# Three transfers for weight sums per half block, begun ahead of DeltaNet's first keys, with the out-projection's groups between those of the pairs

## The chip, the cores and the metric

The kernel runs on one core of a Trainium2 chip. The metric is the device time of one execution in microseconds (us); of several runs the median counts. Engines are named as in the profile: PE is TensorE's matmuls, PEld its weight loads, DVE VectorE, ACT ScalarE, POOL GpSimd, SP SyncE. ACTq and POOLq are the queues through which ScalarE and GpSimd issue transfers; those that GpSimd issues are called software transfers here (q0 on the page).

## The reference

One layer of a hybrid decoder trunk: 512 tokens and 16 meta tokens of width 2048, normalised, go through one input projection, whose columns feed three mixers on disjoint heads; their gated outputs are concatenated and go through one output projection, with a residual and a last norm.

```
h = rms_norm(x, norm_w); h = pad(h)
proj = h @ w_in
dq, dk, dv, dz, db, da, gq, gk, gv, gz, gl, fq, fk, fv, fz, ff = split_cols(proj)
o_dn  = gated_delta_rule_chunked(silu(conv(dq)), silu(conv(dk)), silu(conv(dv)), ...)   # 6 heads x 128
o_gla = gla_chunked(gq, gk, gv, log_g)                                                   # 5 heads
o_fox = forgetting_attention(fq, fk, fv, log_f)                                          # 5 heads x 128
o = concat(gated(o_dn, dz), gated(o_gla, gz), o_fox * silu(fz))
return rms_norm(x + o @ w_out, final_norm_w)
```

## The kernel before, in words

**Projection.** All of x stays on chip, transposed, as a high and a low part (xh, xl). The weights of one head's projection come in two half blocks of 128 x 1024 floats. `load_half` (L145) loads one on SyncE's queue (raw), ScalarE casts it to whi (L166), VectorE takes the rest as wlo (L167), and TensorE multiplies in three parts (whi by xh, whi by xl, wlo by xh; L223). The first four gates (dz) are done in quarters of the weights while x itself still comes in (L265, L277).

**Sums of weights.** For seven pairs of blocks of the forgetting heads (`PAIRS`, L428), and for four groups of the output projection, the kernel multiplies by sums of blocks in place of single blocks, to save products. These sums are formed in DRAM without an engine: software transfers copy a block (L438) or add one to it (L436, an accumulating transfer). A pair fills ti with 4 copies of 256 KB, 2 sums of input weights and 2 sums of ti into ti, the last ones each waiting for earlier ones. A group of the output projection fills tw with the same numbers at 512 KB each. That makes 56 and 32, or 88 transfers. Pairs are numbered from -1 to -7 in the table below, groups of the output projection from 0 to 3.

**What sets the place of the transfers.** `jobs` (L454) appends the transfers of the groups given to it to the list `chores`, stage by stage: first all copies of all groups given, then the first sums, then the others. After each half block `load_half` takes `rate[0]` transfers from the list. The transfers are also ordered behind the split of that half block (`paced`, L171), but only for the program's order; no semaphore makes them wait for it. On the chip a software transfer starts as soon as GpSimd comes to it in its own order and its own waits (for a free slot, or for the transfer that it adds to) are over. `AHEAD` (L1195) is the table: at a point (g, i) of the program, read by `ahead` (L1199), a number sets the rate and a tuple appends groups.

**The stages.** The program goes through DeltaNet's heads in two groups g of three (L1206): gates (`gate_z`), keys (`dn_keys`), values, queries, the inverse of the chunk matrices (`dn_inverse`) and the mix over four blocks (`dn_mix`); then GLA's gates and heads, the five forgetting heads, and the output projection. A point (g, -1) of the table lies between gates and keys, (g, 0) between keys and values. The projections of later stages fill TensorE while the small products of a stage wait for other engines, so inverse and mix of a group lie beside the projections that follow.

**Names and lines that the steps below touch.** In `dn_keys`, gb is a broadcast load of 792 KB on ScalarE's queue, which VectorE reads (L657). In `dn_inverse`, the matrix ab goes to DRAM as sc (L721) and comes back as iv and xm (L724, L726), all three on ScalarE's queue; ScalarE then copies uf (L754). In `dn_mix`, each block loads eg (L834, ScalarE's queue), takes its exponential (L835), copies its last column to egl (L837, VectorE), and multiplies it by q (L838, GpSimd); pks (L842), zz (L845, VectorE), py (L849), y (L851, ScalarE) and psn (L855) follow. In GLA, pss (L983) is a row of 64 tiny products. GpSimd also does the first step of each SiLU (L350: stdz for DeltaNet's gates, stc for its keys, values and queries, stgz for GLA's gates) and memsets (gsc L132 and L133, pb L593, ab L699 and L711, uf L751).

Of the kernel before, what the change touches and what calls it, by code (L numbers as in the profile page):

```python
# [83 lines left out]
def tile_hybrid_trunk(ctx, tc, xT, xtok, mtok, w_gate, w_in, w_out, w_dn, consts, lmask, fin_w, out, dbg=None):  # L84
# [1107 lines left out]

    SUMS = {h: [(h, 0), (h, 1)] for h in range(4)}
    XLAST = 0
    AHEAD = {(0,0):(2,(-1,-2,-3,-4),(-5,-6,-7),(0,1,2,3))}  # L1195
    XSUM = {1: (0,), 2: (1,2), 9:(3,)}
    PM = (308, 319)

    def ahead(g, i):  # L1199
        for n in AHEAD.get((g, i), ()):  # L1200
            if isinstance(n, tuple):
                jobs(*[in_jobs(-k - 1) if k < 0 else out_jobs(k) for k in n])
            else:
                rate[0] = n
# [313 lines left out]
```

## Time and profile before

| | |
|---|---|
| median of 3 runs | 1012.02 us (1011.39 to 1012.87) |
| profiled execution | 1008.45 us |
| its span | 1006.7 us |
| TensorE busy | 988.8 us, 98% |
| VectorE, ScalarE, GpSimd busy | 643.2, 460.5, 247.7 us |
| software transfers (q0) | 31.46 MB, 15.2% of the time of 16 DMA engines |

The span is the time from the first to the last instruction of the profiled execution. In rows of a timeline the first number is the start in us from the span's start, the second the duration, then engine, line, operation, out<-in, and in brackets the idle time of the engine ahead of it with what ended it. In rows of waits stand total, times and longest. In rows of windows stand, after the window, the time span and each engine's busy time with its count of instructions, then the clock granted to TensorE, the DMA engines' busy share, and GB/s.

### The profile page before, as it was taken

The page shows a single profiled execution, that of the slowest core. Times are in us where ns is not written, and L with a number is a line of the kernel's source. Part 1 is how long each engine was busy: PE and PEld are TensorE (multiplying, and loading weights), DVE is VectorE, ACT ScalarE, POOL GpSimd, SP SyncE. Part 2 cuts the span into 40 slices and gives each one's busy share as a digit, 9 for nine tenths or more (in the row PEclk, how much of TensorE's full clock was granted, in tenths as well). Part 3 has the DMA queues.
Part 4 walks back from the last instruction along what each step waited for, and adds up shares of the span by engine and source line. Part 5 has one row for each costly group of instructions (what it writes and reads, how often), then busy time and mean ns, then how long its engine had stood idle before and what let it go on. Part 6 is the DMA issues. An engine that isn't in the chain of part 4 may idle for free.

```text
span 1006.7 us, 19781 instructions
## 1 busy us (share of the span) xinstructions
PE 988.8 (98%) x7866; PEld 906.6 (90%) x7866; DVE 643.2 (64%) x1389; ACT 460.5 (46%) x1041; POOL 247.7 (25%) x280
## 2 busy tenths in 40 slices
PE   9999999999999999998999999999999999999996
PEld 8899999899999888898989988899999998888885
DVE  7366877965566894244576774866474667677673
ACT  7654533434456244143445453555444444444454
POOL 0022533322313334123042620311112123000060
PEclk9999999999999999999999999999999999999999
DMA  9625357655446577456847221243333375457534
GB/s 345 235 67 158 129 174 155 154 137 146 146 118 157 123 213 247 154 122 145 216 107 174 65 74 64 74 137 124 116 117 129 119 241 176 146 168 231 178 114 168
DMA packets 62402, 152.57 MB, mean 152 GB/s; under 512 B 12925, under 2 KB 16173, under 8 KB 62052
## 3 DMA queue, kind: packets, MB, share of 16 engines
q1 hardware_dynamic: 36912, 108.22, 32.5%
q0 software_dynamic: 11136, 31.46, 15.2%
q10 hardware_dynamic: 14260, 11.61, 4.0%
q8 instruction: 62, 1.02, 0.4%
q14 instruction: 32, 0.26, 0.1%
HBM read 143.99 MB, written 38.60 MB: 181 GB/s over the span
## 4 chain that ended last, share of the span: by engine, by line
PE 51%; DVE 2%; issue 0%; ACT 0%; ACTq 0%; DVEq 0%
PE pp L223 13%; PE pp_a L533 6%; PE pa L1295 5%; PE pq L1295 4%; PE pt L1295 4%; PE pp_d L533 3%; PE pp_c L533 3%; PE pp_b L533 3%; PE ps L1295 2%; PE pss L983 1%; PE pr L1295 1%; PE pfo L1186 1%; PE pfa L1153 1%; PE pfx L1170 1%; PE pgo L1046 0%; PE pfd L1154 0%
## 5 line engine op out<-in xcount | busy, mean ns | idle before, releaser
L223 PE MATMUL pp<-xl,whi 128*128 128x264 f32 (+2 forms) x1120 | 284.6, 306 | 0.0
L223 PE MATMUL pp<-xh,whi 128*128 128x264 f32 (+2 forms) x1120 | 282.7, 305 | 1.5 <-DVE fqk L341 0.8
L223 PE MATMUL pp<-xh,wlo 128*128 128x264 f32 (+2 forms) x1120 | 282.6, 305 | 1.4 <-issue 0.9
L223 PEld LDWEIGHTS pp<-xh,whi 128*128 128x128 f32 x1120 | 186.4, 188 | 11.2 <-DVE fqk L341 1.0
L223 PEld LDWEIGHTS pp<-xh,wlo 128*128 128x128 f32 x1120 | 186.6, 189 | 10.7 <-issue 1.4
L223 PEld LDWEIGHTS pp<-xl,whi 128*128 128x128 f32 x1120 | 187.1, 189 | 8.9 <-issue 0.2
L167 DVE TENSOR_TENSOR wlo<-raw,whi 128x1024 fp32r<-128x1024 f32 (+1 forms) x124 | 129.9, 1058 | 87.2 <-ACT whi L166 77.4
L166 ACT CAST whi<-raw 128x1024 fp32r<-128x1024 f32 (+1 forms) x124 | 109.9, 902 | 164.4 <-PE pp L223 122.5
L350 POOL TENSOR_SCALAR stc<-cv 128x528 f32<-128x528 f32 (+1 forms) x18 | 28.1, 1559 | 117.0 <-DVE cv L598 95.5
L598 DVE SCALAR_TENSOR_TENSOR cv<-pb,cpk,cv 128x528 f32<-128x528 f32 (+1 forms) x54 | 41.0, 760 | 0.7
L1319 POOL TENSOR_TENSOR acc<-acc,fw 128x512 f32<-128x512 f32 x4 | 6.3, 1592 | 127.1 <-ACT sqf L1316 127.1
L162 ACT ACTIVATE whi<-raw 128x512 fp32r<-128x512 f32 x35 | 20.5, 624 | 25.3 <-PE pp_c L533 7.9
L166 ACT CAST whis<-raws 128x1024 fp32r<-128x1024 f32 x16 | 16.4, 1049 | 27.4 <-DMA raws<-tw 15.4
L163 DVE SCALAR_TENSOR_TENSOR wlo<-raw,whi 128x512 fp32r<-128x512 f32 x35 | 23.0, 685 | 8.7 <-ACT whi L162 8.6
L1295 PE MATMUL pa<-wloo,oh 128*128 128x512 f32 x72 | 28.4, 395 | 0.0
L1295 PE MATMUL pa<-whio,ol 128*128 128x512 f32 x72 | 28.4, 395 | 0.0
L341 DVE TENSOR_TENSOR pb<-pp,rstd 128x264 f32<-128x264 f32 (+1 forms) x36 | 13.7, 423 | 22.3 <-PE pp L223 22.2
L533 PE MATMUL pp_a<-xh,whi 128*128 128x264 f32 (+1 forms) x112 | 27.9, 282 | 0.0
L533 PE MATMUL pp_a<-xl,whi 128*128 128x264 f32 (+1 forms) x112 | 27.7, 281 | 0.0
L167 DVE TENSOR_TENSOR wlos<-raws,whis 128x1024 fp32r<-128x1024 f32 x16 | 19.3, 1221 | 11.4 <-ACT whis L166 11.4
L1295 PE MATMUL pa<-whio,oh 128*128 128x512 f32 x72 | 25.9, 400 | 0.0
L838 POOL TENSOR_TENSOR eg<-eg,qT 128x384 f32<-128x384 f32 x8 | 8.5, 1058 | 70.2 <-DVE egl L837 70.2
(499 smaller groups left out, 2256.4 us busy)
## 6 DMA issues: line engine op xcount, KB each, us to landing
raw<-in_w_in SPq DMA_DIRECT2D x96, 512.0 KB, 3.9
tw<-in_w_dn POOLq DMA_DIRECT2D x24, 512.0 KB, 6.4
ti<-in_w_in POOLq DMA_DIRECT2D x42, 256.0 KB, 4.7
raw<-ti SPq DMA_DIRECT2D x14, 512.0 KB, 4.1
rawo<-in_w_out SPq DMA_DIRECT2D x13, 512.0 KB, 3.3
raws<-tw SPq DMA_DIRECT2D x12, 512.0 KB, 4.5
raw<-in_w_in SPq DMA_DIRECT2D x21, 256.0 KB, 3.1
xt<-in_xtok SPq DMA_DIRECT2D x8, 512.0 KB, 8.6
```

The costliest lines, as they stand in the source:

```text
L162: pace[0] = A.activation(hi, raw, AF.Copy, scale=-1.0).ins
L163: pace[1] = V.scalar_tensor_tensor(out=lo, in0=raw, scalar=-1.0, in1=hi.bitcast(F32), op0=ALU.mult, op1=ALU.subtract).ins
L166: pace[0] = A.copy(hi, raw).ins
L167: pace[1] = V.tensor_tensor(out=lo, in0=raw, in1=hi.bitcast(F32), op=ALU.subtract).ins
L223: mm = PE.matmul(p_[:, :nt], wt[:, j * m : (j + 1) * m], xx[k][:, t0 : t0 + nt], start=(k == 0 and wt is hi and xx is xh), stop=(k == KT - ...
L341: V.tensor_tensor(out=o, in0=p_[rows], in1=rstd[rows, t0 : t0 + n], op=ALU.mult)
L350: G.tensor_scalar_max(t, src, LOW)
L533: m = PE.matmul(p_[:, cols], wt[:, j * P : (j + 1) * P], xx[j][part_][:, cols], start=first and i == 0, stop=last and i == len(todo) - 1, ...
L598: V.scalar_tensor_tensor(out=c, in0=pb[:, t0 + w : w + T], scalar=cwc[:, blk, w : w + 1], in1=c, op0=ALU.mult, op1=ALU.add)
L983: mm = PE.matmul(ps[o0 : o0 + n, b * n : b * n + n], kx[rr, k0 : k0 + n], qx[rr, q0 : q0 + n], start=True, stop=True)
L1153: PE.matmul(pa[:, :m], qT[:, ts], kT[:, :m], start=True, stop=True)
L1295: PE.matmul(p_, o_[:, s], w_, start=(first and n == 0), stop=(last and n == 2), skip_group_check=True)
```

## The change

```
-    AHEAD = {(0,0):(2,(-1,-2,-3,-4),(-5,-6,-7),(0,1,2,3))}
+    AHEAD = {(0,-1):(3,(-1,-2,-3,-4),(0,1),(-5,-6,-7),(2,3))}
```

The list of transfers is opened ahead of DeltaNet's first keys instead of behind them, six half blocks earlier (the keys of three heads). Three transfers are taken per half block instead of two. The groups stand in another order: pairs -1 to -4, then groups 0 and 1 of the output projection, then pairs -5 to -7, then groups 2 and 3. The transfers themselves are the same 88. The orders of TensorE and SyncE are unchanged; ScalarE and VectorE have neighbours swapped in some places.

GpSimd at the start of the program, before (gsc are the last memsets of the constants, stdz the first gates of DeltaNet, stc its first keys):

```order
L132 MEMSET gsc 128x1
L133 MEMSET gsc 128x4
L350 TENSOR_SCALAR stdz_567<-zdz_564 128x512
L350 TENSOR_SCALAR stdz_576<-zdz_573 128x512
L350 TENSOR_SCALAR stdz_585<-zdz_582 128x512
L350 TENSOR_SCALAR stdz_594<-zdz_591 128x512
L593 MEMSET pb_710 128x3
L350 TENSOR_SCALAR stc_829<-cv_824 128x528
L593 MEMSET pb_835 128x3
L438 DMA ti<-in_w_in 128x512 x2
L350 TENSOR_SCALAR stc_954<-cv_949 128x528
L593 MEMSET pb_960 128x3
```

And after, at the same place:

```order
L132 MEMSET gsc 128x1
L133 MEMSET gsc 128x4
L438 DMA ti<-in_w_in 128x512 x3
L350 TENSOR_SCALAR stdz_567<-zdz_564 128x512
L350 TENSOR_SCALAR stdz_576<-zdz_573 128x512
L350 TENSOR_SCALAR stdz_585<-zdz_582 128x512
L438 DMA ti<-in_w_in 128x512 x2
L350 TENSOR_SCALAR stdz_594<-zdz_591 128x512
L593 MEMSET pb_710 128x3
L438 DMA ti<-in_w_in 128x512 x5
L350 TENSOR_SCALAR stc_834<-cv_829 128x528
L593 MEMSET pb_840 128x3
```

The first copies of ti stood behind the first keys' SiLU; now three stand ahead of the first gate's, behind memsets that wait for no transfer, and ten stand ahead of the first keys'.

GpSimd in the first group's values and queries and the first keys' start of the second group, after (stc are values and queries, stdz gates of the second group, pb the start of its keys; before, transfers of ti stand here):

```order
L438 DMA tw<-in_w_dn 16x8192 x2
L350 TENSOR_SCALAR stc_1957<-cv_1952 128x512
L438 DMA tw<-in_w_dn 16x8192
L711 MEMSET ab_2092 51x32
L436 DMA tw<-in_w_dn 256x512 x4
L350 TENSOR_SCALAR stc_2086<-cv_2081 128x512
L436 DMA tw<-tw 256x512
L350 TENSOR_SCALAR stdz_2703<-zdz_2700 128x512
L436 DMA tw<-tw 256x512 x3
L350 TENSOR_SCALAR stdz_2776<-zdz_2773 128x512
L593 MEMSET pb_2783 128x3
L438 DMA ti<-in_w_in 128x512 x5
```

The first 16 transfers of the output projection's weights, at 512 KB each, have come here from the second group.

GpSimd from the second group's inverse to its mix, before (stgz are GLA's gates, uf and b the inverse's end, kq GLA's first memsets, eg the mix's four blocks):

```order
L350 TENSOR_SCALAR stgz_5029<-zgz_5026 128x512
L751 MEMSET uf_4319 128x1536
L438 DMA tw<-in_w_dn 16x8192 x6
L761 MEMSET b_4349 64x384
L1228 MEMSET kq_5035 128x1536
L1228 MEMSET kq_5036 128x1536
L438 DMA tw<-in_w_dn 16x8192 x2
L838 TENSOR_TENSOR eg_4401<-eg_4401,qT_3749 128x384
L438 DMA tw<-in_w_dn 16x8192
L838 TENSOR_TENSOR eg_4474<-eg_4474,qT_3749 128x384
L436 DMA tw<-in_w_dn 256x512 x3
L838 TENSOR_TENSOR eg_4547<-eg_4547,qT_3749 128x384
```

And after, with the same instructions of the second group:

```order
L350 TENSOR_SCALAR stgz_5057<-zgz_5054 128x512
L751 MEMSET uf_4353 128x1536
L761 MEMSET b_4383 64x384
L1228 MEMSET kq_5063 128x1536
L1228 MEMSET kq_5064 128x1536
L838 TENSOR_TENSOR eg_4435<-eg_4435,qT_3779 128x384
L838 TENSOR_TENSOR eg_4508<-eg_4508,qT_3779 128x384
L838 TENSOR_TENSOR eg_4581<-eg_4581,qT_3779 128x384
```

The transfers between these instructions are gone; the last of all now stands ahead of the second group's inverse, between its two memsets of ab.

## Prediction

> **What bounds the kernel now.** I read the page's first part, then TensorE's own waits, largest first, then engine timelines around each.
>
> ```profile
> span 1006.7 us, 19781 instructions
> PE 988.8 (98%) x7866; PEld 906.6 (90%) x7866; DVE 643.2 (64%) x1389; ACT 460.5 (46%) x1041; POOL 247.7 (25%) x280
> ...
> q0 software_dynamic: 11136, 31.46, 15.2%
> ```
>
> ```profile
> PE py L849 <- DVE zz L845: 2.2, 1, 2.2
> ...
> PE pp L223 <- issue: 0.9, 1, 0.9
> PE pss L983 <- issue: 0.8, 1, 0.8
> ...
> PE pp L223 <- ACT whi L166: 0.7, 1, 0.7
> ...
> PE pp L223 <- DVE wlo L167: 0.5, 1, 0.5
> ```
>
> TensorE is busy for 988.8 of 1006.7 us. The change adds no matmul and takes none away, and the orders of TensorE and SyncE are the same before and after. So it can move the time only by these stalls, or by new ones. None of the 88 software transfers is on the chain that ended last, as their readers, loads of the forgetting heads and of the out-projection, come far later. What counts is **whom the transfers slow down while they run**. They move 31.46 MB in 15.2% of 1006.7 us, that is 153 us at about 205 GB/s.
>
> **What goes: the stalls of the second DeltaNet group.** Before, the 32 out-projection transfers run beside this group's inverse and mix. After, GpSimd's order has its last one ahead of the GLA gates (stgz), and so ahead of the waits that follow. The largest stall is that of py at 461.96 us:
>
> ```profile
> 440.56 0.38 ACTq L834 DMA_DIRECT2D eg<-gd  x1
> 444.05 0.53 ACT L835 ACTIVATE eg<-eg 128x384 f32<-128x384 f32 x1 [0.85 <-DMA eg<-gd]
> ```
>
> ```profile
> 445.89 2.75 POOL L436 DMA_DIRECT2D tw<-in_w_dn  x3
> ```
>
> ```profile
> 453.91 0.37 ACTq L834 DMA_DIRECT2D eg<-gd  x1
> 459.69 0.52 ACT L835 ACTIVATE eg<-eg 128x384 f32<-128x384 f32 x1 [4.91 <-DMA eg<-gd]
> ```
>
> ```profile
> 455.00:460.00 5.00, 4.80 (x42) 4.59 (x40) 0.00 (x0) 0.31 (x1) 0.00 (x0) 1.00 0.89 235
> ```
>
> The same load of eg takes 444.05 - 440.56 = 3.49 us in one block and 459.69 - 453.91 = 5.78 us in the next, when three accumulating copies of 512 KB are in flight and the DMA engines are busy to 0.89. VectorE's copy egl waits for it, zz stands behind egl in VectorE's order, and py waits for zz. The load is 2.29 us late and the stall is 2.2. Without the transfers **2.2 us** go; 0 if the delay has another cause.
>
> The next pair, whi 0.7 and wlo 0.5, stands where that group's inverse ends:
>
> ```profile
> 206.49 0.26 ACTq L721 DMA_DIRECT2D sc<-ab  x1
> 211.74 0.40 ACTq L724 DMA_DIRECT2D iv<-sc  x1
> ...
> 385.15 0.26 ACTq L721 DMA_DIRECT2D sc<-ab  x1
> ...
> 393.60 0.38 ACTq L724 DMA_DIRECT2D iv<-sc  x1
> ```
>
> ```profile
> 385.43 0.98 POOL L438 DMA_DIRECT2D tw<-in_w_dn  x2
> ```
>
> ScalarE stands at L724 until sc has landed: 211.74 - 206.49 = 5.25 us in the first group, 393.60 - 385.15 = 8.45 us here, with two copies of 512 KB issued 0.3 us after it. The gate's activations, the copies of uf and the cast of whi queue up behind. With 3.2 us back the cast is in time, and **1.2 us** go (0 to 1.2).
>
> Last the two stalls whose releaser is "issue":
>
> ```profile
> 513.57 0.39 PE L223 MATMUL pp<-xh,wlo 128*128 128x264 f32 x1 [0.86 <-issue]
> ...
> 518.32 0.32 PE L983 MATMUL pss<-kq,kq 64*32 64x32 f32 x20 [0.77 <-issue]
> ```
>
> ```profile
> 506.51 1.79 POOL L436 DMA_DIRECT2D tw<-tw  x2
> ```
>
> TensorE waits there for nothing that the profile shows, among 64 tiny matmuls at a time, with two 512 KB accumulating copies in flight. If its instructions came late because of these, both go (1.6 us); if not, none. I take half, **0.8 us**. The other rows of this view lie at the very start or among the later heads, where no software transfer runs before or after; they stay.
>
> **What comes: three copies at the very start.** The first three 256 KB copies of ti now stand on GpSimd right behind the memsets of gsc, ahead of the first activation step, and wait for nothing.
>
> ```profile
> 2.45 0.13 POOL L133 MEMSET gsc<- 128x4 bf16 x1
> 54.38 4.40 POOL L350 TENSOR_SCALAR stdz<-zdz 128x512 f32<-128x512 f32 x3 [51.80 <-DVE zdz L362]
> ```
>
> ```profile
> 0.00:5.00 5.00, 3.80 (x18) 3.80 (x19) 0.35 (x1) 2.40 (x3) 1.82 (x18) 1.00 0.61 170
> 5.00:10.00 5.00, 5.00 (x26) 4.37 (x26) 3.02 (x5) 2.79 (x6) 0.00 (x0) 1.00 0.98 334
> ```
>
> ```profile
> 7.36 0.62 ACT L166 CAST whi1q<-raw1q 128x512 fp32r<-128x512 f32 x1 [0.45 <-DMA raw1q<-in_w_in]
> 8.69 0.74 ACT L265 ACTIVATE xh<-xs,cpk 128x528 fp32r<-128x528 f32 x1 [0.71 <-DMA xs<-in_xT]
> ```
>
> ```profile
> 6.48 0.63 PE L277 MATMUL pp<-xh,wlo0q 128*128 128x512 f32 x1
> ...
> 8.30 0.40 PE L277 MATMUL pp<-xh,whi1q 128*128 128x512 f32 x1
> ...
> 10.14 0.39 PE L277 MATMUL pp<-xh,whi0q 128*128 128x512 f32 x1
> ```
>
> So they issue from 2.6 us on, into DMA engines that are soon full (0.61, then 0.98) and feed a TensorE that waits for them. 3 x 262 KB = 786 KB at 334 GB/s take 2.35 us from the loads of x and of the first weights. The cast of whi1q ends at 7.98 us and its matmul starts at 8.30: 0.32 us of slack. The xh that is ready at 9.43 us is read at 10.14: 0.71 us. So of 2.35 us, some 0.4 is absorbed: **+1.9 us**, since this stage keeps TensorE full to its end and gives nothing back. Lower bound 0.3: the three copies get only the gaps of the first 5 us, where the engines are busy to 0.61. Upper bound 4: the first matmuls take 0.63 us where later ones take 0.39, and a longer wait among the first may bring that back.
>
> What a turn between the queues would make of it: if the loads keep half of each engine while the copies run, they have lost 1.7 us by the cast at 7.36 (half of 3.4 us, if they begin at 4 us) and all 2.35 by 9.4, and less the slacks that is 1.4 and 1.6 us instead of 1.9. The Trainium skill, "DMA: Bandwidth & Descriptors" (Queues, rings and completion order), states such a rule: each DMA engine goes round the queues that it has work for and changes after a packet. No row here shows whose packet goes first, and I stay with 1.9.
>
> **What comes: a denser first group.** The 44 half blocks of transfers become 30, and the out-projection's first 16 now lie in the first DeltaNet group. GpSimd's own issue time (2.75 us for three sums, in the row above) delays the gates and values that stand behind it by less than the slacks below, and is set at nothing; without those it would be some 1 us at a place. The early places with little slack are these:
>
> ```profile
> 89.36 0.50 DVE L657 TENSOR_SCALAR atm<-gb,gcol 16x16 f32<-16x16 f32 x3 [1.06 <-DMA gb<-gd]
> ...
> 93.49 1.21 DVE L167 TENSOR_TENSOR wlo<-raw,whi 128x1024 fp32r<-128x1024 f32 x1
> ```
>
> ```profile
> 97.59 0.40 PE L223 MATMUL pp<-xh,wlo 128*128 128x264 f32 x2
> ...
> 183.72 0.40 PE L223 MATMUL pp<-xh,whi 128*128 128x512 f32 x1
> ...
> 309.75 0.38 PE L849 MATMUL py<-zz,uf 128*128 128x128 f32 x2
> ```
>
> ```profile
> 306.93 0.86 DVE L845 SCALAR_TENSOR_TENSOR zz<-pks,cols,vp 128x128 f32<-128x128 f32 x3
> ```
>
> ```profile
> 178.79 1.05 ACT L166 CAST whi<-raw 128x1024 fp32r<-128x1024 f32 x1 [5.17 <-DMA raw<-in_w_in]
> ...
> 183.69 1.05 ACT L166 CAST whi<-raw 128x1024 fp32r<-128x1024 f32 x1 [1.25 <-PE pp L223]
> ...
> 304.95 0.52 ACT L835 ACTIVATE eg<-eg 128x384 f32<-128x384 f32 x1 [0.51 <-DMA eg<-gd]
> ```
>
> - gb at 89 us: VectorE waits for it, and the split wlo stands behind. TensorE reads that wlo at 97.6 us, 2.9 us after its end at 94.7. Six copies and a sum are in flight where there were two copies.
> - the weights cast at 178.8 us, which land just then: four accumulating copies of 512 KB now run beside them. Their matmul starts at 183.7, 3.9 us after the cast ends.
> - sc at 206 us: three accumulating copies of tw and then five of ti are now near it. At 3.2 us more, as at 385 us, the casts behind it are just in time.
> - eg at 305 us: five copies of 512 KB now stand there. At 2.29 us more, as at 454 us, it eats a slack of 2 us: zz ends at 307.8 us, py starts at 309.75.
>
> Each is between 0 (the slack holds) and 1.8 us: the worst delay seen, 3.2 us, half as much again because three transfers run where two did, less a slack of 3. All four lie nearer to nothing, since each slack about equals the delay seen: 0.3 us each, **+1.2 us**.
>
> Sum: 1.9 + 1.2 - 2.2 - 1.2 - 0.8 = -1.1 us on the span, 1005.6. The profiled execution took 1008.45 us, 1.75 more than its span and 3.57 less than the median of the runs, 1012.02; against that median the forecast is **1010.9 us**.
>
> **The rivals.** About 0.2%, or 2 us, is what a measurement of this kernel can tell from no change.
> - **The start is free and the late stalls go.** The early copies take the gaps, the four places hold. 0.3 - 2.2 - 1.2 - 1.6 = -4.7: 1007.3 us. For it: the DMA engines have 0.39 of the first 5 us free. Against it: 0.98 right after.
> - **The crowded first group starves TensorE.** Mechanism: the latency-bound loads eg, gb and sc wait behind denser software traffic, as eg did at 454 us, and with slacks of 2 to 3 us each delay over 3 us is a stall. It decides once three transfers per half block pile up: three of 512 KB take 7.7 us at 205 GB/s, and the casts of two half blocks start 4.9 us apart (178.79 and 183.69). Then three of the four places cost their 1.8 beside the start's 1.9 and the 4.2 that go: 5.4 + 1.9 - 4.2 = +3.1, **1015.1 us**; with all four and the start at 4 us, 1019.0.
> - **Nothing changes on the path.** The start absorbs the copies (0.3) and the late stalls have other causes (egl's place in VectorE's order, ScalarE's queue), and come back: 1012.3 us.
>
> **How the numbers follow.** The forecast (each term within about 1 us, 1009 to 1013) gets 0.40, the free start 0.22, the crowded group 0.28, nothing 0.10. Faster by over 2 us (below 1010.0): all of the free start and a third of the forecast, 0.36. Slower by over 2 us (above 1014.0): nearly all of the crowded group and a little of the forecast, 0.30. Within: 0.34. The range takes in the free start with the spread of its terms and the crowded group up to the middle of its two times: 1006.7 to 1016.5.
>
> **What would show it.** The first three ti copies issue before 5 us, and the matmul of whi1q starts near 10 us; the first work of GpSimd behind them, at 54.4 us before, starts 1.9 us later. The wait of py for zz is gone, eg lands in 3.5 us in every block of the second group, L724 follows L721 by 5 us there, and the "issue" stalls at 513 and 518 us are gone or, if they are not, had nothing to do with transfers. New waits of TensorE for wlo near 97 us, whi near 183 and 217 us or zz near 309 us are the crowded group's. The forecast is wrong if the first stage is not delayed, or if one of these is over 1 us.

## The result and the profile after

The changed kernel takes **1020.46 us** (median of 6 runs, 1019.06 to 1021.98) against 1012.09 us of the kernel before (6 runs, 1009.19 to 1015.17): a ratio of 1.0084, 95% interval 1.0063 to 1.0104. It is slower by about 8.4 us, where 1.1 us less was forecast. The ratios here and below are those of the comparison with its interval, and can differ a little from the quotient of the medians. The profiled execution is that of 1019.06 us.

The page's head and TensorE's own waits, after (total, times, longest):

```profile
span 1017.4 us, 19780 instructions
PE 993.1 (98%) x7866; PEld 908.3 (89%) x7866; DVE 641.1 (63%) x1389; ACT 460.7 (45%) x1041; POOL 249.5 (25%) x280
...
q0 software_dynamic: 11136, 31.46, 14.9%
```

```profile
PE pm L735 <- DVE iv L729: 4.3, 2, 3.9
PE pss L983 <- issue: 1.9, 1, 1.9
PE pp L277 <- ACT whi2q L166: 1.6, 1, 1.6
PE pp L223 <- DVE wlo L167: 1.2, 3, 0.5
```

The software transfers move the same bytes in the same share of time. The wait of py is gone from the list, as forecast. At its head stands one that the list of before didn't have: pm, which waits for iv, in the first group's inverse. TensorE's busy time is also up by 4.3 us, with the same 7866 matmuls.

Since TensorE's order is the same in both kernels, each matmul can be set against its twin, and the difference of their start times, from one span's start to the other's, is a step curve that shows where the 10.6 us came from (the medians differ by 8.4: the profiled execution of before lies 3.6 us under its median, that of after 1.4 under its own):

```
place in the kernel (us of before)         steps, us    sum, us
start, casts of whi1q and whi2q (8 to 11)    +2.40       +2.40
pk behind gb (100 to 122)                    +1.08       +3.48
pm, first inverse (221 to 232)               +6.45       +9.95
mix of the first group (235 to 345)          +0.20      +10.15
whi, wlo, second inverse (348 to 388)        +2.37      +12.52
whi, wlo at 400                              -0.23      +12.29
py and what is near it (430 to 474)          -1.90      +10.39
GLA's pss (513 to 518)                       +0.13      +10.52
the rest                                     +0.12      +10.64
```

**The first inverse.** ScalarE's and VectorE's timelines there, after; the answering rows of before are 206.49 and 211.74:

```profile
213.44 0.26 ACTq L721 DMA_DIRECT2D sc<-ab  x1
...
219.34 0.40 ACTq L724 DMA_DIRECT2D iv<-sc  x1
```

```profile
227.51 0.58 DVE L729 STREAM_TRANSPOSE iv<-iv 128x384 f32<-128x384 f32 x1 [9.44 <-DMA iv<-sc]
```

```profile
216.59 1.62 POOL L438 DMA_DIRECT2D ti<-in_w_in  x3
219.37 1.39 POOL L751 MEMSET uf<- 128x1536 f32 x1 [1.15 <-DMA sc<-ab]
220.69 1.04 POOL L438 DMA_DIRECT2D ti<-in_w_in  x2
```

```profile
228.14 1.49 PE L735 MATMUL pm<-iv,an 32*32 32x32 f32 x48 [3.86 <-DVE iv L729]
```

iv comes back 227.51 - 219.34 = 8.17 us after its load is issued, with five copies of ti in flight from GpSimd's rows; before, the transpose starts at 214.41 us, 2.67 us behind its load. The trip begins late, too: L721 stands 6.95 us later than before, 3.5 of which the whole kernel was late by then. Altogether iv is 9.6 us later than that shift, and TensorE waits 3.86 us for it. The windows right behind (2 us each; the last three numbers are the granted clock, the DMA share and GB/s) show what the wait costs beyond itself:

```profile
226.00:228.00 2.00, 0.00 (x0) 0.00 (x0) 0.49 (x1) 0.00 (x0) 0.00 (x0) 0.76 0.08 24
228.00:230.00 2.00, 1.86 (x50) 1.79 (x51) 1.85 (x8) 1.79 (x4) 0.00 (x0) 0.50 0.00 0
230.00:232.00 2.00, 2.00 (x11) 2.00 (x11) 1.96 (x4) 1.19 (x3) 0.00 (x0) 0.50 0.00 0
232.00:234.00 2.00, 2.00 (x11) 2.00 (x11) 1.43 (x2) 0.00 (x0) 0.38 (x1) 0.53 0.90 246
```

Behind the idle stretch the clock that TensorE was granted is at half up to about 234 us, nearly 6 us after pm has started, and this gives the other 2.5 of the step's 6.45 us.

**The start.** GpSimd issues the three copies at 2.49 us, and whi2q comes late:

```profile
2.49 1.87 POOL L438 DMA_DIRECT2D ti<-in_w_in  x3
56.79 4.42 POOL L350 TENSOR_SCALAR stdz<-zdz 128x512 f32<-128x512 f32 x3 [52.42 <-DVE zdz L362]
```

```profile
12.84 0.50 PE L277 MATMUL pp<-xh,whi2q 128*128 128x512 f32 x1 [1.60 <-ACT whi2q L166]
```

stdz starts at 56.79 instead of 54.38 us: the 2.4 us stay to the end of the stage. The next step is gb, which VectorE had at 89.36 us before:

```profile
94.12 0.50 DVE L657 TENSOR_SCALAR atm<-gb,gcol 16x16 f32<-16x16 f32 x3 [3.42 <-DMA gb<-gd]
```

**The second inverse and mix.** The inverse's first trip (L702 to L707 on ScalarE's queue) and the eg that had been late, after:

```profile
348.75 1.98 ACTq L702 DMA_DIRECT2D scr<-an  x4
350.84 0.28 ACTq L708 DMA_DIRECT2D ab<-scmeta  x1
357.65 0.32 ACTq L707 DMA_DIRECT2D ab<-scr  x1
358.02 1.99 ACT L166 CAST whi<-raw 128x1024 fp32r<-128x1024 f32 x2 [12.83 <-DMA scr<-an]
```

```profile
344.85 0.89 POOL L436 DMA_DIRECT2D tw<-tw  x1 [1.95 <-DMA tw<-tw]
349.90 0.88 POOL L436 DMA_DIRECT2D tw<-tw  x1 [2.84 <-DMA tw<-tw]
```

```profile
466.40 0.37 ACTq L834 DMA_DIRECT2D eg<-gd  x1
470.11 0.52 ACT L835 ACTIVATE eg<-eg 128x384 f32<-128x384 f32 x1 [2.84 <-DMA eg<-gd]
```

L707 follows L702 by 8.90 us, where it was 5.54 before (338.60 to 344.14), with the last two 512 KB sums of tw in flight; two casts of weights stand behind it on ScalarE. That is a place that the prediction didn't have. The eg is back at 3.71 us, and py no longer waits.

### The profile page after: what moved, and what is told of

Its sections match the earlier page's. It is cut to its first block, busy times and chain, and to the rows that moved or that the text cites. A ratio compares the mean times of both kernels' runs of the same rounds, so it can differ in the third digit from the quotient of the medians.

```text
span 1017.4 us, 19780 instructions
## 1 busy us (share of the span) xinstructions
PE 993.1 (98%) x7866; PEld 908.3 (89%) x7866; DVE 641.1 (63%) x1389; ACT 460.7 (45%) x1041; POOL 249.5 (25%) x280
## 4 chain that ended last, share of the span: by engine, by line
PE 51%; DVE 2%; issue 0%; ACT 0%; ACTq 0%; DVEq 0%
PE pp L223 13%; PE pp_a L533 6%; PE pa L1295 5%; PE pq L1295 4%; PE pt L1295 4%; PE pp_d L533 3%; PE pp_c L533 3%; PE pp_b L533 3%; PE ps L1295 2%; PE pss L983 1%; PE pr L1295 1%; PE pfo L1186 1%; PE pfa L1153 1%; PE pfx L1170 1%; PE pgo L1046 0%
## 5 line engine op out<-in xcount | busy, mean ns | idle before, releaser
L350 POOL TENSOR_SCALAR stc<-cv 128x528 f32<-128x528 f32 (+1 forms) x18 | 30.6, 1699 | 120.2 <-DVE cv L598 96.3
L162 ACT ACTIVATE whi<-raw 128x512 fp32r<-128x512 f32 x35 | 20.5, 624 | 25.4 <-PE pp_c L533 10.6
L351 ACT ACTIVATE stc<-stc 128x528 f32<-128x528 f32 (+1 forms) x18 | 11.5, 638 | 33.0 <-POOL stc L350 21.0
```

Source lines behind the costliest of these rows:

```text
L162: pace[0] = A.activation(hi, raw, AF.Copy, scale=-1.0).ins
L350: G.tensor_scalar_max(t, src, LOW)
L351: A.activation(t, t, AF.Exp, scale=-1.0)
```

## The experiments

**The theory**: the time is lost where small loads on ScalarE's queue make a round trip (ab, sc and iv of the inverses, gb, eg) while software transfers are in flight, and at the start. **Rivals**: the early opening shifts everything and is the whole cause; the rate of three is; the out-projection's new place is; the neighbours that swapped on VectorE are (splits of weights that moved ahead of inverse steps).

Medians in us, ratios to the kernel before with intervals. "Step" means the step curve of the run's profile against the first profile of before; where TensorE's order differs a little from that of before, the matmuls are set against each other by their position.

### One part of the change at a time

```
a1_early    AHEAD = {(0,-1):(2,(-1,-2,-3,-4),(-5,-6,-7),(0,1,2,3))}
a2_rate3    AHEAD = {(0,0):(3,(-1,-2,-3,-4),(-5,-6,-7),(0,1,2,3))}
a3_order    AHEAD = {(0,0):(2,(-1,-2,-3,-4),(0,1),(-5,-6,-7),(2,3))}
a4_nostart  AHEAD = {(0,0):(3,(-1,-2,-3,-4),(0,1),(-5,-6,-7),(2,3))}
```

a1_early, expected: 

> The kernel before with the list opened ahead of the first keys, but still two transfers per half block and the groups in the old order. Theory (round trips: the change loses time where small latency-bound loads on ScalarE's queue run beside software transfers, plus the copies at the very start): two copies of 256 KB at the start cost two thirds of the 2.4 us that three cost, +1.6; the inverse of the first group sees two transfers per half block as before, so its stall of 4 us and more does not come, 0 to +2; the stalls of the second group stay. In all +1.5 to +4 us. Rival (the early opening is the whole cause, since everything behind is shifted): +8 to +10 us. Rival (the rate of three is the cause): within 0.5 us of before.

Measured: **1007.51, ratio 0.9949 (0.9928 to 0.9970): faster than before**. Steps: +1.08 at the start, +1.4 near 100 us, +1.7 at pm of the second inverse, then -2.2 at py and -1.0 at 513 us. The early opening alone is no loss; that rival falls. The theory's own forecast for this run, 1.5 to 4 us slower, was missed too: it had left the stalls of py and at 513 us in place.

a2_rate3, expected: 

> The kernel before with three transfers per half block, opened behind the first keys as before, old order. Theory (round trips): no copies at the start, 0; ten copies of ti stand around the return of iv in the first group's inverse, so TensorE's wait for pm near 221 us comes, +3 to +6; the waits for py at 462 us and at 400 us go, -2 to -3.3. In all +0 to +4 us. Rival (early opening is the cause): -2 to -3 us. Rival (the place of the out-projection's groups is the cause): -2 to -3 us.

Measured: 1017.31, ratio 1.0045 (1.0027 to 1.0063). That is about 4.6 us, a little above the expected 0 to 4, and the place was not the expected one: the first inverse's trip stayed at 5.3 and 2.7 us, with next to nothing in flight beside it. Instead +1.8 at 173 us, +3.2 at py of the first mix (290 us, eg 8.75 us on its way), +8.1 at the second inverse's first trip (L702 to L707 11.0 us), and -2.3 at the old py. So at a rate of three, in the old order, stalls come; where they come depends on which transfers stand beside which trip.

a3_order, expected: 

> The kernel before with only the order of the groups changed: out-projection 0 and 1 ahead of pairs -5 to -7, two per half block from behind the first keys. Theory (round trips): nothing changes up to 240 us, so no stall at the first inverse; 512 KB transfers then run beside the first group's mix (eg), where slack is 2 us, 0 to +2; transfers of 256 KB run beside the second inverse and mix, where 512 KB ones did, so that the 2.2 us of py shrink, 0 to -2. In all -2 to +2 us. Rival (the place of the out-projection's groups is the cause): +5 to +10 us.

Measured: 1011.28, ratio 0.9999 (0.9978 to 1.0020). The first inverse is untouched (+0.2 up to 260 us), the first mix loses 2.0 (eg 7.21 us on its way), pm of the second inverse 1.4, and py gives back 2.3. The new order alone is no loss either.

a4_nostart, expected: 

> The changed kernel with the list opened behind the first keys as before, so that no copy stands at the start; three per half block and the new order stay. Theory (round trips): the 2.4 us of the start and most of the 1.1 us at 100 us go; the first inverse's return leg now has eight 512 KB copies beside it, worse than the 256 KB copies of the changed kernel, so its stall stays, +4 to +8; the second group's stalls stay away, -2 to -3. In all +2 to +6 us against before. Rival (early opening is the cause): -3 to 0 us against before.

Measured: 1013.24, ratio 1.0004 (0.9988 to 1.0020). The start's loss is gone, as expected; 1.5 us come at 173 to 179 us, and the splits around the first inverse cost 2.2 us instead of 4 to 8. The return leg took 3.58 us, with only the first 0.6 us of one 512 KB sum beside it: the eight copies of the expectation weren't there. (This profile also loses 3.3 us in the output projection near 930 to 945 us, where no software transfer runs; why is open.) So the same rate and order cost 8 us with the opening six half blocks earlier (2.4 of them the start's), and without it between -1.2 and +2.0 us. The opening and the order are harmless alone, the rate alone costs 4.6 us in the old order: the theory is that what decides is what stands beside the trips, and the next runs try that.

### Taking the suspect away

```
b1_hold   the changed kernel; nothing taken in half blocks 25 to 28 from the opening on (counted from 1)
-        for _ in range(rate[0]):
+        for _ in range(TAKE.get(chores and seen.append(0) or len(seen), rate[0])):
+    TAKE = {25: 0, 26: 0, 27: 0, 28: 0}
b5_start  the same with TAKE = {1: 0, 2: 6}
```

b1_hold, expected: 

> The changed kernel, but for four half blocks no transfer is taken from the list, so that none stands on GpSimd between the second gate and the second key of the second group, where iv comes back in the first inverse; all later transfers move back by four half blocks. Theory (round trips): iv lands again in 2 to 3 us instead of 8, and the wait of pm for iv at 228 us and what follows it, together 6.4 us, goes down to 0 to 2; the stall of 1.8 us at 359 us may change either way, since other transfers stand there. In all 4 to 7 us faster than the changed kernel, 1013 to 1016 us. Rival (order of VectorE: the splits that moved ahead of the inverse's steps delay it): no change, 1019 to 1021 us.

Measured: **1015.14, ratio 1.0031 (1.0010 to 1.0051)**, 5.3 us under the changed kernel's median. Its ScalarE and VectorE rows:

```profile
216.39 0.26 ACTq L721 DMA_DIRECT2D sc<-ab  x1
...
222.08 0.40 ACTq L724 DMA_DIRECT2D iv<-sc  x1
```

```profile
225.32 0.58 DVE L729 STREAM_TRANSPOSE iv<-iv 128x384 f32<-128x384 f32 x1 [5.30 <-DMA iv<-sc]
```

The return leg is back at 3.24 us, pm doesn't wait, and the step at the first inverse is 0.7 instead of 6.45. L721 itself is still late. (All later transfers move back by four half blocks, too. At the start, which is the changed kernel's, this profile loses 4.0 us instead of 2.4: TensorE waits 1.09 us for whi2q at 12.84 us, and the clock is at 0.50 from 14 to 16 us.) The splits of weights that moved on VectorE stand where the change put them ahead of the inverse, so that rival doesn't make the stall.

b5_start, expected: 

> The changed kernel, but the first three copies, which stood ahead of the first gates, are issued with the next two, behind three gates; all else stands where it stood. Theory (shared DMA engines): the 2.4 us of the start go, all other stalls stay: 2 to 2.6 us faster than the changed kernel, 1017.5 to 1018.5 us. Rival (the start's stall is the clock or chance): no change.

Measured: 1018.54, ratio 1.0056 (1.0039 to 1.0073), 1.9 us under the changed kernel. Its profile has no step at the start, and the wait of pm (4.8 us) as before. The start's term is the three copies'.

### Adding the suspect to the kernel before

```
d1_burst  the kernel before; xx is a scratch tile in DRAM; at the 20th half block, ahead of that half block's own transfers:
+    chores.insert(0, steps_of([(0, xx[i], w_in[2 * i + 1, 0][:, :KC]) for i in range(10)]))
```

d1_burst, expected: 

> The kernel before, and ten more copies of 256 KB, whose results nobody reads, issued behind the first keys' memset of the second group at about 198 us, beside the return trip of the first inverse. Nothing else moves. Theory (round trips): L721 to L724 goes from 5.3 to 7 to 10 us and L724 to the transpose of iv from 2.7 to 3 to 6 us, so that iv comes 3 to 7 us later, and after a slack of some 5.7 us TensorE's wait for pm is 0 to 1.5 us, with up to 2 more at the casts behind L724. Rival (the trip's length has to do with the order of the queues, not with the traffic): both legs within 0.5 us of before.

Measured: 1020.83 in one run, against 1011.16 of before. ScalarE's queue, GpSimd, TensorE and two windows (4 us each) of this run:

```profile
206.55 0.26 ACTq L721 DMA_DIRECT2D sc<-ab  x1
...
219.14 0.40 ACTq L724 DMA_DIRECT2D iv<-sc  x1
```

```profile
199.14 4.00 POOL L438 DMA_DIRECT2D xx<-in_w_in  x7
204.81 0.53 POOL L438 DMA_DIRECT2D xx<-in_w_in  x1 [1.66 <-DMA ti<-ti]
205.51 1.12 POOL L438 DMA_DIRECT2D xx<-in_w_in  x2 [0.17 <-issue]
```

```profile
221.70 0.51 PE L223 MATMUL pp<-xh,whi 128*128 128x264 f32 x2 [3.41 <-ACT whi L166]
224.40 0.81 PE L223 MATMUL pp<-xh,wlo 128*128 128x264 f32 x2 [1.74 <-DVE wlo L167]
```

```profile
222.00:226.00 4.00, 2.26 (x11) 1.95 (x10) 3.96 (x8) 3.23 (x6) 2.69 (x5) 0.51 0.54 75
226.00:230.00 4.00, 4.00 (x64) 3.72 (x63) 2.87 (x5) 0.39 (x1) 0.87 (x1) 0.64 1.02 219
```

L721 to L724 takes 12.59 us instead of 5.25, with an identical L721. ScalarE stands at L724 and the cast of whi behind it; TensorE idles 3.41 us, its clock falls to half, and the curve is 7.9 us higher at 230 us. So one burst of ten plain copies beside this trip costs about as much as the whole change. (The curve rises by 4.0 us more between 460 and 520 us, with the eg of 462 us 6.27 us on its way; that part wasn't followed up.) The size was underestimated (up to 3.5 expected), for the cast behind L724 has less slack than iv, and for the clock.

### A second look at the kernel before

c0_again is the kernel before, unchanged. Expected: 

> The kernel before, unchanged, for a second profile. The profile of before lay 3 us under the median of its runs. Theory: the same places stall in every run by other amounts, so that this profile shows the waits of py, whi and wlo again, each within 1.5 us of the first, and its span is between 1007 and 1011 us. Rival: the difference lies in some place that the first profile doesn't show at all.

Measured: 1009.84 in one run, span 1008.0. The curve is flat within 0.3 us up to 390 us, then +0.9 at pm near 397 us; py waits as before. So the places hold from run to run. The two profiled executions of before lie 3.6 and 2.1 us under the medians of the runs taken with them (1012.09 and 1011.89), and which place makes up the rest is not settled; step curves against the first profile are therefore up to 3.6 us less kind than the medians.

### Where else the transfers can go

```
x_late      AHEAD = {(0,0):(2,(-1,-2,-3,-4),(-5,-6,-7)),("g",0):((0,1,2,3),)}
z1_afterdn  AHEAD = {(0,0):(2,(-1,-2,-3,-4),(-5,-6,-7)),("g",2):(3,(0,1,2,3))}
```

x_late, expected: 

> The kernel before with the four groups of the output projection opened only ahead of GLA's first pair of heads, so that no software transfer stands beside the second DeltaNet group's inverse and mix; rate 2 and the start as before. Theory (round trips): the waits of py (2.2) and of whi and wlo (1.2) go, nothing comes in the first group: 3 to 4 us faster than before, 1007.5 to 1008.5 us. Rival (these stalls have other causes): no change, 1011 to 1012 us.

Measured: 1012.58, ratio 1.0010 (0.9995 to 1.0025). The run didn't do what it was meant to: GLA's first point lies ahead of the second inverse in the program, and the copies began at 380 us instead of 368. So L721 to L724 was 9.43 us long, and pm waited 1.9 us. No software transfer was in flight beside the eg that had been late (3.38 us on its way), and py's 2.3 us went. So the half of the expectation about py held; the half about whi and wlo isn't tested by it.

z1_afterdn, expected: 

> The kernel before, but the four groups of the output projection are opened at GLA's last pair of heads, three per half block, so that they run from about 475 us on; before that point only the pairs' transfers run, as before. The run x_late was meant to do this, but its transfers began only two half blocks later than before's and still lay beside the second inverse and mix. Theory (round trips): with nothing in flight L724 follows L721 by 5.0 to 5.4 us in the second group and eg lands in 3.1 to 3.8 us, so the waits of py (2.2) and of whi, wlo or pm near 400 us (1.3) go; the waits called issue stay (1 to 2 us); GLA's own stage may take up to 1.5 us for the moved transfers. In all 2 to 3.5 us faster than before, 1008 to 1010 us. Rival (the second group's stalls come from the order of the engines' queues): the waits stay, 1011 to 1013 us.

Measured: 1012.93, ratio 1.0008 (0.9995 to 1.0022). The theory's first half holds, in ScalarE's rows of the second group:

```profile
386.07 0.26 ACTq L721 DMA_DIRECT2D sc<-ab  x1
...
391.93 0.38 ACTq L724 DMA_DIRECT2D iv<-sc  x1
```

5.86 us instead of 8.45; whi, wlo and py no longer wait, and the curve is at -2.9 us at 480. Then, with the copies from 503.5 us on, GLA gives back 9 us, where 1.5 at most were expected. TensorE, and a window behind:

```profile
512.09 0.39 PE L223 MATMUL pp<-xh,wlo 128*128 128x264 f32 x1 [2.39 <-issue]
...
567.43 0.63 PE L983 MATMUL pss<-kq 64*32 64x32 f32 x42 [3.45 <-issue]
...
574.45 0.85 PE L983 MATMUL pss<-kq,gqk 64*32 64x32 f32 x63 [1.59 <-issue]
```

```profile
568.00:572.00 4.00, 4.00 (x84) 3.72 (x81) 1.32 (x5) 0.00 (x0) 0.00 (x0) 0.61 1.09 262
```

The stalls called "issue" among the 64 tiny products of pss grow with the traffic beside them: at the second pair of heads (565 to 575 us) there is none before, with no software transfer there, 1.6 us in x_late, and 5.0 us plus a half-speed clock here. At the first pair (513 to 518 us) they stand in every profile, 1.0 to 2.4 us, with traffic or without. The packet records of the traces say more: each of the 19 stalls of this kind in GLA, in all 14 profiles, ends 1.2 to 1.6 us behind the end of a 16 KB packet of the queue that the page calls "q8 instruction". Here these packets end at 510.57, 566.05 and 573.00 us, and the stalls at 512.09, 567.43 and 574.45. That fits a TensorE that waits for its instructions; no run took these packets away.

### A version that is faster than both

a1_again, expected: 

> a1_early once more, with more rounds, since its median was 4 us under before's while its profile showed 1.3 us more stall than the profile of before. Theory: the early opening at two per half block ends the transfers about 30 us earlier, so that the waits of py and at 513 us (3.2 us) go for 2.2 to 3.5 us of new ones ahead of 110 us and a longer one for iv at 400 us: 0 to 3 us faster than before. Rival (the 4 us were chance): within 1 us of before.

Measured: 1007.42 (12 runs), ratio 0.9961 (0.9948 to 0.9973): the gain is no chance.

```
y1_best   a1_early with TAKE = {1: 0, 2: 4, 48: 4, 49: 4, 51: 0, 52: 0}
```

y1_best, expected: 

> a1_early (opened ahead of the first keys, two per half block, old order) without two of the things that still cost there: the first two copies are issued with the next two, behind three gates, and the three copies of 512 KB beside the second group's L721 to L724 are taken in two earlier half blocks instead. Theory (round trips and start): the start's 0.9 to 1.1 us go, L721 to L724 of the second group goes from 7.5 to 8.7 us down to 5.0 to 5.9, so the wait of pm for iv near 400 us (0.6 to 1.8 us) goes; all else stays. In all 1 to 2.5 us faster than a1_early, 1005 to 1006.5 us, and faster than both kernels of the change. Rival (the earlier bunch of four copies costs as much where it stands now): within 0.7 us of a1_early.

Measured: **1004.55, ratio 0.9916 (0.9887 to 0.9945)**, 7.8 us under before in the same comparison and a little better than forecast. GpSimd around the second group's trip, and ScalarE's queue:

```profile
359.21 2.46 POOL L438 DMA_DIRECT2D tw<-in_w_dn  x5
370.24 1.99 POOL L438 DMA_DIRECT2D tw<-in_w_dn  x4
394.87 5.50 POOL L436 DMA_DIRECT2D tw<-in_w_dn  x6
```

```profile
387.91 0.26 ACTq L721 DMA_DIRECT2D sc<-ab  x1
...
393.51 0.38 ACTq L724 DMA_DIRECT2D iv<-sc  x1
```

With nothing issued between 372 and 394 us the trip takes 5.60 us and pm doesn't wait; the start has no step. All 88 transfers are there, and in the old order.

### All profiles together

The length of the trips, with what was in flight beside them:

```
second group, L721 to L724   nothing:  after 5.11, a4 5.27, b1 5.28, b5 5.30, y1 5.60, a2 5.67, z1 5.86
                             1 or 2 copies of tw:  a1 7.49 and 8.71, before 8.45, d1 8.58, c0 9.40, x_late 9.43
                             2 sums of ti:  a3 6.66
first group, L721 to L724    next to nothing:  4.97 to 5.31 in nine profiles, b1 5.69
                             3 copies of ti:  after 5.90, b5 7.53;  10 copies:  d1 12.59;  2 sums of tw:  a4 5.14
L724 to iv's transpose       next to nothing, or transfers just issued:  2.6 to 3.6
                             5 copies of ti:  b5 4.53, after 8.17;  6 sums of ti:  a3 (second group) 5.11
second group, L702 to L707   next to nothing:  2.9 to 4.1 in nine profiles;  2.1 us of a copy of tw:  a4 4.2
                             sums of tw:  b5 7.3, after 7.5, b1 8.5, a2 11.0
eg, issue to its activation  nothing:  3.0 to 3.9
                             sums or copies, over 2 us of them in all:  3.5 to 7.2, a2 8.75
```

(L702 is taken at its last issue here; the first of the four is 1.4 to 4.0 us earlier.) One row is an exception: in a4 two sums of tw were in flight beside most of the first group's L721 to L724, and it took 5.14 us. What in the memory or the queues makes the small loads wait was not separated.

## Why the prediction was wrong, point by point

- **What bounds the kernel**: right. TensorE does the same work in the same order; all of the difference is its waits, and the half-speed clock behind some of them.
- **The start, +1.9**: right in mechanism, and +2.40 in size (4.0 in b1_hold's profile, with a stretch at half clock that the term didn't have). Nothing was absorbed. b5_start shows it to be the three copies.
- **py, -2.2**: right. It went, with 3.71 us for eg. (Of the three copies that the prediction saw in flight beside it, the first had landed before that eg was issued.)
- **whi and wlo at 400 us, -1.2**: only -0.23. The trip did fall to 5.11 us and whi's wait went, but wlo's stayed (0.52 us), and pm ahead of them came 0.27 us later. In z1_afterdn both went, so the mechanism is right.
- **"issue", -0.8**: +0.13. The stall at the first pair stays without any transfer; elsewhere in GLA transfers can make such stalls (z1_afterdn). Half was neither. The copies that the prediction put beside both stalls had landed by 515.3 us, ahead of the one at 518 us.
- **gb, +0.3**: gb came at 94.12 us, 2.4 us later than the start's shift, and pk and what follows cost 1.08 us: mis-sized, within the bound of 1.8.
- **whi at 179 us and eg at 305 us, +0.3 each**: 0, and 0.2 in the whole mix.
- **sc at 206 us, +0.3, at most 1.8: this is the step that failed**, as the prediction put it: "At 3.2 us more, as at 385 us, the casts behind it are just in time." It was +6.45. Three things were left out. I priced one leg, L721 to L724, which was only 0.65 us longer; but the inverse makes a chain of trips, whose delays add: the first came 2.6 us late (VectorE's first step on ab at 175.13 instead of 169.00 us, less the 3.5), VectorE's steps 0.8, and the return of iv 5.5, which I hadn't listed. Second, GpSimd's order: in the changed kernel's rows stc and three copies of ti come before uf, which waits for sc. Before, uf came first, and the transfers behind it started at 214.73 us, when iv was back (214.41). So nothing held the copies off the late trip (read from the rows, not tried by itself; in b1_hold stc stands ahead of uf as well, without copies, and there is no stall). Third, behind the wait of 3.9 us the clock came down. b1_hold takes the copies beside the return leg away, and all but 0.7 us of the step with them.
- **The second inverse's first trip, +2.4 in all**: not in the prediction, though it is the same chain on the same queue, with the last sums of tw beside it.
- **The count of half blocks** was wrong: an emptied entry of the list uses up a take too, 44 of them beside the 88 transfers. The list lasts 66 half blocks at two and 44 at three, not 44 and 30. The order that was used was right, as it is the program's own.
- **The rivals**: "the crowded first group" came nearest, and its mechanism, small loads that wait behind denser traffic, is the one that the runs bear out. Its places were not: of the four only gb (1.08) and sc (6.45) cost, and TensorE's wait at sc was that of pm for iv, which it didn't name. Its price at 1015.1 us, and its worst at 1019.0, was too low, and its chance of 0.28 was too small. Its threshold (three transfers of 512 KB take longer than a half block) wasn't what decided: a2_rate3 had no stall at the first inverse at a rate of three, and d1_burst has a large one at two.

## What to carry to other kernels

The same 88 transfers, in the same 15% of the time, cost by their neighbours: list every small round trip on the path with its slack, as chains and not one by one, and keep the background out of just those windows. When pricing a stall of over 1 us, allow for a stretch at half clock behind it. And when a change moves traffic, ask not only which trips it leaves but which it lands on; here the same rate and order cost 8 us or nothing that can be told, by six half blocks of shift, and the same 88 transfers, opened early and kept out of two windows, gave 7.8 us.

## What the runs showed of the hardware that was not expected

- A wait of 3.86, 3.41 or 3.45 us was followed by windows at a granted clock of 0.50, 0.51 and 0.61. Shorter waits did it too, but not always: 1.09 us (b1_hold, 0.50 behind it), 1.81 (a1_early, below) and 2.39 (z1_afterdn at 512 us, 0.51), while waits of 1.86 (after, at 528.83 us), 2.16 (before, py) and 2.42 us (a2_rate3, at 294 us) left it at 1.00. So the length of one wait doesn't decide it here. The Trainium skill, "TensorE: Matmul & The Clock Gate" (Part 1: The HAM clock gate), gives an idle window of about 3.4 us as the point from which TensorE falls to half its clock. The three long waits agree with that figure; the shorter ones don't.

```profile
401.08 0.95 PE L735 MATMUL pm<-iv,an 32*32 32x32 f32 x48 [1.81 <-DVE iv L729]
```

```profile
403.00:405.00 2.00, 2.00 (x11) 2.00 (x10) 0.71 (x1) 1.95 (x4) 1.96 (x3) 0.52 1.11 192
```

- TensorE can stand idle in a way that the profile calls "issue": 64 products of 32 columns take 0.76 us, and beside 512 KB copies that stage waited 5.0 us where it waited for nothing without them. The stalls end 1.2 to 1.6 us behind a packet of "q8 instruction". That the copies delay these packets is a guess; no run separates it.
- Plain copies of 256 KB within DRAM, ten issued beside it, made one trip of 204 KB on another queue take 12.6 us instead of 5.25.
